# Reordered token loads, paired modulation products and rearranged feed-forward buffers in a hybrid pooling and attention layer

## The chip, the cores and the metric

The kernel runs on one core of one Trainium2 chip. The metric is device time in microseconds (us) of one execution: 905.08 us before the change, the median of 3 runs (904.38 to 905.84).

## The reference, cut to what matters

One layer works on 640 tokens of width 1024: 128 context tokens (`x_prompt`) and 512 latent tokens (`x_sample`, a grid of 8 rows by 64 columns). All numbers are fp32.

```python
shift, scale, gate = split(silu(cond) @ w_mod + b_mod)    # two conditions: latent and context
h = rms(x) * g * (1 + scale) + shift
z = h @ w_in                                  # pooling channels, q, k, v and two gates
x1 = x + gate * ((pool_branch * sigmoid_a + attention_branch * sigmoid_b) @ w_out)
h2 = rms(x1) * g2 * (1 + scale2) + shift2
u = h2 @ w_up                                 # 2 x 2816 features
cv = conv3(u)                                 # width-3 depthwise convolution over tokens
y = x1 + gate2 * ((silu(cv[:, :2816]) * cv[:, 2816:]) @ w_down)
```

The outputs are y for both kinds of tokens and the new k and v of the context.

## The kernel before, in words

There are 128 partitions. Channels come in 8 tiles of 128 (`kt`), tokens in 5 tiles of 128 (`t`; tile 0 is the context, tiles 1 to 4 are latent), features in 22 tiles (`f`). An fp32 operand is split into a high part (a cast to fp32r on ScalarE) and a low part (operand minus high part, on VectorE); a product is three matmuls: high times high, high times low, low times high. The helper `split_to` (L132 to L134) makes the pair: L133 is the cast, L134 the subtraction. A tile scheduler sets each engine's order from the program's order and its own estimate of when things are due; `tc.keep_in_program_order`, `tc.issue_after` and `add_manual_dep` pin single instructions.

The stages, by where they lie in the trace:

- **0 to 140 us, start and projections.** `load_x` (L254) loads the token tiles: the context contiguously (L256), the latent tiles through `xl_blocks` (L251), which gives partition p of a block the tokens of a 16-column strip of the grid: from one grid row to the next the address moves on by 64 tokens, 256 KB. `normalise` (L271) squares and sums a tile on ScalarE (L275), takes the root (L277) and the reciprocal (L279), scales (L280), and TensorE transposes it (L284). `mod_rows` (L142) makes shift and scale for one channel tile: two weight tiles `in_wm` of 512 KB, 8 matmuls by the condition `cz` (L149) into one PSUM tile, and a copy to `mrows` (L152); `mod_scale_shift` (L155) turns the rows into columns with two products by the two-column selector `sel` (L157, L158). `make_h` (L292) writes the modulated h^T, split. The v product runs over the channel tiles (`tok_step`, L203 to L205). The raw weight tiles here share `SRAW` = 6 buffers.
- **140 to 400 us.** Attention, pooling, gates and merge. The change does not touch their code.
- **400 to 457 us, output projection and second norm.** `out_product(t)` (L727) makes the second half of the output columns for token tile t (L745 to L747); `residual` (L717) multiplies by the gate, adds to `x1` and squares. The row statistics follow (L751 to L754); `xn` is x1 times the reciprocal root (L756, ScalarE, 128x1024, one buffer). `second_h(t-1)` (L762) is called in the middle of the product of tile t: 8 transposes of `xn` against the identity (L768), 8 modulations from PSUM (L773 on ScalarE, L776 on VectorE), splits into `b1h`, `b1l` and others. `second_h(4)` stands behind the last product. `sums` (L796) forms differences of quarters of h2^T in three pieces.
- **457 to 850 us, feed-forward.** h2^T is a 2 by 2 block matrix, and for f from 1 on 7 block products take the place of 8, at the price of sums of weights (`weight_sums`, L817, four 128x512 operations on GpSimd) and of activations. `plain` makes f = 0, `up_a` and `up_b` with `products_b` the others (all their matmuls are L865). The convolution (L953 to L955) uses the buffers `ua` (2) and `ug` (1). A group of two f's is multiplied by the down weights (`down_group`, L998; matmuls L994 to L996). `down_weights` (L977) loads 512 KB tiles into `raw`, three buffers shared with the up weights, and splits them into `dhi` and `dlo`.
- **850 to 903 us, the last four f's.** `down_last` (L1010) works through 11 pieces of the output. Each loads its x1 from DRAM into one of three `xr` buffers (L1029) and takes three steps: PSUM plus `acc` (L1031), times the gate `gfb` (L1032), plus `xr` (L1033; pieces 0 to 6 on GpSimd, the others on VectorE), then the store (L1035).

Of the kernel before, what the change touches and what calls it, by code (L numbers as in the profile page):

```python
# [36 lines left out]
SRAW = 6  # L37
# [3 lines left out]
MID = 4  # L41
CUT = 256
# [22 lines left out]
def body(ctx, tc, A):  # L65
# [22 lines left out]
    sel = const.tile([P, 2], F32, name="sel")  # L88
# [42 lines left out]

    def split_to(raw, hi, lo):  # L132
        nc.scalar.copy(hi, raw)  # L133
        return nc.vector.tensor_tensor(out=lo, in0=raw, in1=hi.bitcast(F32), op=SUB)  # L134
# [7 lines left out]
    def mod_rows(chunk, rp):  # L142


        ps = ps_small()
        for half in range(2):
            r = load_raw(A["wm"][2 * chunk + half], rp)
            for k4 in range(4):
                nc.tensor.matmul(ps[32 * k4:32 * k4 + 32, :256], lhsT=cz[:, half * 4 + k4, :],  # L149
                                 rhs=r[:, k4 * 256:(k4 + 1) * 256], start=(half == 0), stop=(half == 1))  # L150
        rows = rp.tile([P, 256], F32, tag="mrows", name="mrows", bufs=2)
        nc.scalar.copy(rows, ps[:, :256])  # L152
        return rows

    def mod_scale_shift(kt, rows):  # L155
        ps = ps_small()
        nc.tensor.matmul(ps[:, 0:2], lhsT=rows[:, :P], rhs=sel, start=True, stop=True)  # L157
        nc.tensor.matmul(ps[:, 2:4], lhsT=rows[:, P:], rhs=sel, start=True, stop=True)  # L158
        nc.vector.tensor_scalar(out=mS[:, 0, kt, :], in0=ps[:, 0:2], scalar1=vec[:, V_BSA + kt:V_BSA + kt + 1],
                                scalar2=None, op0=ADD)  # L160
        nc.vector.tensor_scalar(out=mA[:, 0, kt, :], in0=ps[:, 2:4], scalar1=bca1[:, kt:kt + 1],
                                scalar2=vec[:, V_GM + kt:V_GM + kt + 1], op0=ADD, op1=MULT)
# [87 lines left out]

    xl_blocks = A["xl"].rearrange("(r t c) d -> t c r d", r=ROWS, c=16)  # L251
    junk = hlo.rearrange("p a b -> p (a b)")

    def load_x(t):  # L254
        if t == 0:
            nc.sync.dma_start(xts[0], A["xc"])  # L256
        else:
            nc.sync.dma_start(xts[t], xl_blocks[t - 1])
# [4 lines left out]
    def split_wv():  # L263
# [3 lines left out]
        tc.keep_in_program_order(nc.scalar.copy(hi, r))  # L267
        nc.gpsimd.tensor_tensor(out=lo, in0=r, in1=hi.bitcast(F32), op=SUB)
# [34 lines left out]
    rows = {0: mod_rows(0, sp)}  # L303
    for t in range(3):
        load_x(t)
    rows[0] = mod_scale_shift(0, rows[0])
# [11 lines left out]
    rows[1] = mod_rows(1, sp)  # L318
    make_h(0, done * P, T)
    mod_scale_shift(1, rows.pop(1))  # L320
    acc = ps_five()
    for kt in range(KT):
        if kt % 2 == 1 and kt < KT - 1:
            split_wv()
        if kt + 2 < KT:
            rows[kt + 2] = mod_rows(kt + 2, sp)
        if kt % 2 == 0 and kt < KT - 2:
            load_wv()
        if kt + 1 < KT:
            make_h(kt + 1)  # L330
        if kt + 2 < KT:
            mod_scale_shift(kt + 2, rows.pop(kt + 2))
# [383 lines left out]

    def residual(ps, t, chunk, sq):  # L717
# [5 lines left out]
        else:  # L723
            nc.vector.tensor_tensor(out=x1[:, t, sl], in0=x1[:, t, sl], in1=tmp, op=ADD)
        nc.scalar.activation(tmp, x1[:, t, sl], AF.Square, accum_out=sq[:, t:t + 1])
# [13 lines left out]
    def out_product(t, mid):  # L739
# [13 lines left out]
        nc.scalar.activation(std, std, AF.Sqrt, bias=eps, scale=1.0 / D)  # L753
        nc.vector.reciprocal(std, std)  # L754
# [7 lines left out]
    def second_h(t, xn):  # L762
# [71 lines left out]
    for t in range(5):  # L834
        xns.append(out_product(t, lambda t: second_h(t, xns[t])))
        if t == 3:
            sums(*J[0])
# [312 lines left out]
```

## Time and profile before

| | |
|---|---|
| median of 3 runs | 905.08 us |
| the profiled execution | 904.5 us |
| its span in the trace | 902.7 us |
| TensorE matmul (PE) | 864.6 us, 96% of the span |
| TensorE weight load (PEld) | 778.1 us, 86% |
| VectorE (DVE) | 663.9 us, 74% |
| ScalarE (ACT) | 394.3 us, 44% |
| GpSimd (POOL) | 227.1 us, 25% |
| DMA | 112.20 MB, mean 124 GB/s |

PE is TensorE's matmuls, PEld its weight loads, which overlap them; SPq is the DMA queue that SyncE issues into. The trace names an instruction by its line, its engine, the tile written and the tiles read, and gives the idle time before it with what ended that.

### The profile page before, as it was taken

The page shows a single profiled execution, that of the slowest core. Times are in us where ns is not written, and L with a number is a line of the kernel's source. Part 1 is how long each engine was busy: PE and PEld are TensorE (multiplying, and loading weights), DVE is VectorE, ACT ScalarE, POOL GpSimd, SP SyncE. Part 2 cuts the span into 40 slices and gives each one's busy share as a digit, 9 for nine tenths or more (in the row PEclk, how much of TensorE's full clock was granted, in tenths as well). Part 3 has the DMA queues.
Part 4 walks back from the last instruction along what each step waited for, and adds up shares of the span by engine and source line. Part 5 has one row for each costly group of instructions (what it writes and reads, how often), then busy time and mean ns, then how long its engine had stood idle before and what let it go on. Part 6 is the DMA issues. An engine that isn't in the chain of part 4 may idle for free.

```text
span 902.7 us, 13356 instructions
## 1 busy us (share of the span) xinstructions
PE 864.6 (96%) x5234; PEld 778.1 (86%) x5234; DVE 663.9 (74%) x1003; ACT 394.3 (44%) x711; POOL 227.1 (25%) x176
## 2 busy tenths in 40 slices
PE   3999999999998999999999899999999999999897
PEld 2778898887898999987799799999989999898885
DVE  2657986897479733544799778879797887978767
ACT  4441245444443323223775553535445353444540
POOL 2121000000000021322016423354332444423304
PEclk9999999999999999999999999999999999999999
DMA  9859425674364222255213321213222121312206
GB/s 252 304 195 272 138 77 176 199 227 135 100 206 158 84 79 73 71 214 183 95 46 138 131 74 67 94 47 99 89 94 88 53 94 50 127 59 94 94 0 198
DMA packets 33023, 112.20 MB, mean 124 GB/s; under 512 B 3856, under 2 KB 4528, under 8 KB 32704
## 3 DMA queue, kind: packets, MB, share of 16 engines
q1 hardware_dynamic: 31840, 107.91, 35.9%
q0 software_dynamic: 1120, 3.44, 1.3%
q8 instruction: 41, 0.67, 0.3%
q14 instruction: 22, 0.18, 0.1%
HBM read 104.50 MB, written 5.78 MB: 122 GB/s over the span
## 4 chain that ended last, share of the span: by engine, by line
PE 82%; DVE 7%; DMA 5%; ACT 3%; issue 2%; SPq 0%; POOL 0%; DVEq 0%; ACTq 0%; POOLq 0%
PE acc L865 25%; PE acc L219 21%; PE sm L995 5%; PE sm L996 5%; PE sm L994 4%; PE acc L203 4%; PE acc L205 4%; PE acc L204 4%; DVE wlo L134 2%; DMA raw<-in_wdn 2%; DMA na<-in_xl 2%; ACT whi L133 2%; PE sm L543 1%; PE sm L527 1%; PE sm L505 1%
## 5 line engine op out<-in xcount | busy, mean ns | idle before, releaser
L133 ACT CAST whi<-raw 128x1024 fp32r<-128x1024 f32 (+1 forms) x86 | 81.2, 946 | 192.8 <-PE acc L865 84.3
L134 DVE TENSOR_TENSOR wlo<-raw,whi 128x1024 fp32r<-128x1024 f32 (+1 forms) x86 | 102.5, 1192 | 37.5 <-ACT whi L133 36.6
L865 PE MATMUL acc<-th,whi 128*128 128x322 f32 (+1 forms) x336 | 103.8, 313 | 4.3 <-ACT whi L133 3.0
L865 PE MATMUL acc<-tl,whi 128*128 128x322 f32 (+1 forms) x336 | 104.5, 311 | 0.0
L865 PE MATMUL acc<-th,wlo 128*128 128x322 f32 (+1 forms) x336 | 104.2, 311 | 0.0
L219 PE MATMUL acc<-hhi,whi 128*128 128x320 f32 x320 | 91.0, 318 | 0.4 <-ACT t L442 0.4
L219 PE MATMUL acc<-hlo,whi 128*128 128x320 f32 x320 | 88.9, 311 | 0.0
L219 PE MATMUL acc<-hhi,wlo 128*128 128x320 f32 x320 | 88.1, 311 | 0.0
L819 POOL TENSOR_TENSOR ws<-raw 128x512 f32<-128x512 f32 x21 | 31.3, 1493 | 199.1 <-DMA raw<-in_wup 88.5
L995 PE MATMUL sm<-dlo,ahi 128*128 128x512 f32 (+1 forms) x188 | 73.9, 393 | 0.3 <-DVE dlo L134 0.3
L994 PE MATMUL sm<-dhi,ahi 128*128 128x512 f32 (+1 forms) x188 | 71.2, 394 | 2.5 <-ACT dhi L133 2.5
L996 PE MATMUL sm<-dhi,alo 128*128 128x512 f32 (+1 forms) x188 | 71.4, 394 | 0.0
L865 PEld LDWEIGHTS acc<-th,whi 128*128 128x128 f32 x336 | 63.0, 189 | 7.5 <-ACT whi L133 5.0
L865 PEld LDWEIGHTS acc<-tl,whi 128*128 128x128 f32 x336 | 63.4, 189 | 1.5
L865 PEld LDWEIGHTS acc<-th,wlo 128*128 128x128 f32 x336 | 63.3, 189 | 1.1
L133 ACT CAST whi<-ws 128x1024 fp32r<-128x1024 f32 x42 | 43.0, 1046 | 41.8 <-PE acc L865 41.7
L1008 DVE TENSOR_TENSOR acc<-sm,acc 128x512 f32<-128x512 f32 x80 | 53.3, 683 | 9.5 <-PE sm L996 9.2
L219 PEld LDWEIGHTS acc<-hhi,whi 128*128 128x128 f32 x320 | 57.7, 189 | 2.8 <-issue 1.5
L219 PEld LDWEIGHTS acc<-hlo,whi 128*128 128x128 f32 x320 | 57.6, 188 | 0.8 <-issue 0.7
L865 PE MATMUL acc<-b1h,whi 128*128 128x322 f32 x184 | 57.4, 316 | 0.5 <-ACT b1h L133 0.5
L219 PEld LDWEIGHTS acc<-hhi,wlo 128*128 128x128 f32 x320 | 57.1, 188 | 0.7 <-issue 0.5
L134 DVE TENSOR_TENSOR wlo<-ws,whi 128x1024 fp32r<-128x1024 f32 x42 | 51.6, 1248 | 8.2 <-ACT whi L133 8.2
(295 smaller groups left out, 2244.7 us busy)
## 6 DMA issues: line engine op xcount, KB each, us to landing
raw<-in_wup SPq DMA_DIRECT2D x44, 512.0 KB, 4.0
mw<-in_wmT SPq DMA_DIRECT2D x32, 512.0 KB, 4.2
raw<-in_wdn SPq DMA_DIRECT2D x22, 512.0 KB, 3.6
raw<-in_wmt SPq DMA_DIRECT2D x20, 512.0 KB, 3.5
raw<-in_wm SPq DMA_DIRECT2D x16, 512.0 KB, 4.6
raw<-in_wtok SPq DMA_DIRECT2D x12, 512.0 KB, 7.9
bias<-in_bias SPq DMA_DIRECT2D x16, 384.0 KB, 3.7
raw<-in_wab SPq DMA_DIRECT2D x8, 512.0 KB, 3.5
```

The lines of the kernel that those rows point to most:

```text
L133: nc.scalar.copy(hi, raw)
L134: return nc.vector.tensor_tensor(out=lo, in0=raw, in1=hi.bitcast(F32), op=SUB)
L203: nc.tensor.matmul(ps[t], lhsT=xh, rhs=wh, start=(kt == 0), stop=False)
L204: nc.tensor.matmul(ps[t], lhsT=xh, rhs=wl, start=False, stop=False)
L205: nc.tensor.matmul(ps[t], lhsT=xl, rhs=wh, start=False, stop=(kt == KT - 1))
L219: nc.tensor.matmul(o[:, :n], lhsT=w[:, k], rhs=cut(x, k, c, n), start=st and a, stop=sp and b)
L819: first = nc.gpsimd.tensor_tensor(out=s[:, 1], in0=a21, in1=a22, op=ADD).ins
L865: upped[0] = nc.tensor.matmul(ps[:, cs], lhsT=a[:, c], rhs=b[:, k, cs], start=start and first, stop=last, skip_group_check=skip and not st ...
L994: nc.tensor.matmul(ps, lhsT=xh, rhs=hi[:, sl], start=first and j == js[0], stop=False)
L995: nc.tensor.matmul(ps, lhsT=xh, rhs=lo[:, sl], start=False, stop=False)
L996: nc.tensor.matmul(ps, lhsT=xl, rhs=hi[:, sl], start=False, stop=last and j == js[-1])
L1008: nc.vector.tensor_tensor(out=o, in0=ps, in1=o, op=ADD)
```

## The change

- **Token loads.** The host lays the latent tokens out once more as `xb`, in the column order of h^T, so that each tile is one contiguous 512 KB block; the loads keep program order, and the context and the first latent tile go ahead of the modulation weights. `SRAW` goes from 6 to 9. `split_wv` works in halves.
- **Modulation by pairs.** Channel tiles 0 and 1 stay single. From tile 2 on two tiles share one PSUM tile, one copy and two four-column products; `sel` grows to 6 columns.
- **Second norm.** In place of `xn` and its transposes, ScalarE writes the diagonal matrix `dg` (identity times the reciprocal root, 128x128, two buffers), and the product of x1 and `dg`, an fp32 matmul, transposes and scales at once. `second_h(4)` moves into `plain`'s second product. The sums come in two pieces, one of 64 and one of 258 columns. `behind` adds order between instructions without a semaphore.
- **Weight sums** for f = 2 and 3 move from GpSimd to VectorE.
- **Buffers of the feed-forward.** `ug` gets two buffers. The down weights get a buffer of their own, `dr` (one); the last four alternate between `dr` and `raw`, and their casts go behind the last cast of `up_w`.
- **Last pieces.** All 11 pieces of x1 are loaded ahead into `b1h` and `b1l`, behind the last load of `dr`. The pieces from 6 on have `acc` times gate plus x1 formed on VectorE before their matmuls are done; then PSUM times gate and one addition finish them. Pieces 0 to 5 keep three steps, the third on GpSimd.

```diff
-SRAW = 6
+SRAW = 9
+PRE = 6
...
-    def mod_rows(chunk, rp):
-        ps = ps_small()
+    def mod_rows(c0, n, rp):
+        ps, m = ps_small(), 4 // n
         for half in range(2):
-            r = load_raw(A["wm"][2 * chunk + half], rp)
+            rs = [load_raw(A["wm"][2 * (c0 + j) + half], rp) for j in range(n)]
             for k4 in range(4):
-                nc.tensor.matmul(ps[32 * k4:32 * k4 + 32, :256], lhsT=cz[:, half * 4 + k4, :],
-                                 rhs=r[:, k4 * 256:(k4 + 1) * 256], start=(half == 0), stop=(half == 1))
+                for j, r in enumerate(rs):
+                    g = 32 * (m * j + k4 % m)
+                    nc.tensor.matmul(ps[g:g + 32, :256], lhsT=cz[:, half * 4 + k4, :],
+                                     rhs=r[:, k4 * 256:(k4 + 1) * 256], start=half == 0 and k4 < m,
+                                     stop=half == 1 and k4 >= 4 - m)
...
-            nc.sync.dma_start(xts[t], xl_blocks[t - 1])
+            tc.keep_in_program_order(nc.sync.dma_start(xts[t], A["xb"][t - 1]))
...
-        xn = fp.tile([P, D], F32, name="xn2", bufs=1)
-        nc.scalar.activation(xn, x1[:, t, :], AF.Copy, scale=std)
-        return xn
+        dg = fp.tile([P, P], F32, name="dg", bufs=2)
+        chain["diagonal"] = nc.scalar.activation(dg, ident, AF.Copy, scale=std).ins
+        return dg
...
-                nc.tensor.transpose(pt[:, k * P:(k + 1) * P], xn[:, (q * 4 + k) * P:(q * 4 + k + 1) * P], ident)
+                i = nc.tensor.matmul(pt[:, k * P:(k + 1) * P], lhsT=x1[:, t, (q * 4 + k) * P:(q * 4 + k + 1) * P],
+                                     rhs=dg, start=True, stop=True).ins
...
+        eng = nc.vector if f in (2, 3) else nc.gpsimd
...
-us = {n: [fw.tile([P, TC], F32, name=f"u{n}{j}") for j in range(b)] for n, b in (("a", 2), ("g", 1))}
+us = {n: [fw.tile([P, TC], F32, name=f"u{n}{j}") for j in range(2)] for n in "ag"}
...
-            r = load_raw(A["wdn"][g * GRP + j])
+            if g < NG - 1 or j % 2 == 0:
+                r = fr.tile([P, D], F32, name="dr", bufs=1)
+                loaded[0] = nc.sync.dma_start(r, A["wdn"][g * GRP + j]).ins
+            else:
+                r = load_raw(A["wdn"][g * GRP + j])
...
+        for i, (t, c, w) in enumerate(pieces):
+            behind(nc.sync.dma_start(place(i)[2], xscr[:, t, c:c + w]).ins, loaded[0])
...
+        for i in range(PRE, len(pieces)):
+            o, gate, x = place(i)
+            behind(nc.vector.tensor_tensor(out=o, in0=o, in1=gate, op=MULT).ins, split_last[0])
+            nc.vector.tensor_tensor(out=o, in0=o, in1=x, op=ADD)
...
-            xr = fr.tile([P, 512], F32, tag="xr", name="xr", bufs=3)[:, :w]
-            nc.sync.dma_start(xr, xscr[:, t, sl])
-            o = acc[:, t, sl]
-            nc.vector.tensor_tensor(out=o, in0=ps, in1=o, op=ADD)
-            nc.vector.tensor_tensor(out=o, in0=o, in1=gfb[:, 1 if t == 0 else 0, sl], op=MULT)
-            (nc.gpsimd if i < 7 else nc.vector).tensor_tensor(out=o, in0=o, in1=xr, op=ADD)
+            o, gate, x = place(i)
+            if i < PRE:
+                nc.vector.tensor_tensor(out=o, in0=ps, in1=o, op=ADD)
+                nc.vector.tensor_tensor(out=o, in0=o, in1=gate, op=MULT)
+                nc.gpsimd.tensor_tensor(out=o, in0=o, in1=x, op=ADD)
+            else:
+                tmp = fr.tile([P, AC], F32, name="cv", bufs=3)[:, :w]
+                nc.vector.tensor_tensor(out=tmp, in0=ps, in1=gate, op=MULT)
+                nc.vector.tensor_tensor(out=o, in0=o, in1=tmp, op=ADD)
```

How the order of instructions moves, at three places (a row names the line, the operation, the tile written and what it reads; x2 is a repeat):

On SyncE's queue at the start, before (`vv` and `na` hold the token tiles, `raw` the weights):

```order
L87 DMA vec<-in_vec 128x262
L126 DMA raw<-in_wm 128x1024 x2
L256 DMA vv<-in_xc 128x1024
L258 DMA vv<-in_xl 128x1x1024 x2
L126 DMA raw<-in_wtok 128x1024
L258 DMA na<-in_xl 128x1x1024 x2
```

The same queue after the change:

```order
L88 DMA vec<-in_vec 128x262
L267 DMA vv<-in_xc 128x1024
L269 DMA vv<-in_xb 128x1024
L127 DMA raw<-in_wm 128x1024 x2
L269 DMA vv<-in_xb 128x1024
L127 DMA raw<-in_wtok 128x1024
L269 DMA na<-in_xb 128x1024 x2
```

Two token tiles now stand ahead of the first two modulation weights; the last two stay behind the first tile of v's weights.

On ScalarE in the steady state (one group of down weights, as it repeats), after the change (`dhi` is the high part of a down weight, `dr` its single raw buffer):

```order
L140 CAST dhi<-dr 128x1024
L140 CAST whi<-raw 128x1024
L981 ACTIVATE cv<-ua_4535,vec 128x642
L936 COPY u_6037<-acc 128x320
L140 CAST dhi<-dr 128x1024
```

Three instructions lie between the two casts that use `dr`, where before the casts read from three buffers.

On ScalarE near the end, before:

```order
L970 ACTIVATE cv<-cv 128x642
L133 CAST dhi<-raw 128x1024
L889 COPY p_8219<-acc 128x322
L133 CAST dhi<-raw 128x1024
L133 CAST whi<-ws 128x1024
L133 CAST whi_8309<-ws 128x1024
```

After the change:

```order
L1000 ACTIVATE cv<-cv 128x642
L906 COPY p_8200<-acc 128x322
L140 CAST whi<-ws 128x1024
L140 CAST whi_8290<-ws 128x1024
L939 COPY p_8235<-acc 128x320
L140 CAST ahi<-cv 128x642
L981 ACTIVATE cv<-ua_4534,vec 128x642
L936 COPY u_8315<-acc 128x320
L1000 ACTIVATE cv<-cv 128x642
L140 CAST whi_8298<-raw 128x512
L140 CAST dhi<-dr 128x1024
L140 CAST dhi<-raw 128x1024
```

The casts of the last down weights now stand behind the casts of the summed weights `ws` instead of ahead of them.

## Rows read from the trace of the kernel before

**Rows 1.** Page, busy time, share and instructions of each engine.

```profile
PE 864.6 (96%) x5234; PEld 778.1 (86%) x5234; DVE 663.9 (74%) x1003; ACT 394.3 (44%) x711; POOL 227.1 (25%) x176
```

**Rows 2.** Waits of PE: line, tile, releaser: us in total, times, longest us.

```profile
PE sm L149 <- DMA raw<-in_wm: 7.3, 2, 5.2
...
PE acc L865 <- ACT whi L133: 3.0, 3, 2.4
PE sm L994 <- ACT dhi L133: 2.5, 1, 2.5
...
PE sm L768 <- ACT xn L756: 1.8, 1, 1.8
PE acc L865 <- DVE wlo L134: 1.7, 1, 1.7
PE acc L865 <- DVE ug L920: 1.3, 1, 1.3
...
PE sm L768 <- ACT hf L773: 1.0, 1, 1.0
```

**Rows 3.** Windows: stretch, us, busy (x) PE PEld DVE ACT POOL, clock, DMA share, GB/s.

```profile
9.00:21.00 12.00, 7.02 (x35) 5.63 (x28) 5.66 (x13) 6.12 (x12) 1.33 (x2) 1.00 1.04 244
21.00:27.00 6.00, 3.95 (x15) 3.39 (x16) 2.88 (x7) 3.83 (x9) 2.02 (x2) 0.73 1.03 379
...
453.00:457.00 4.00, 3.88 (x15) 3.71 (x16) 4.00 (x11) 4.00 (x10) 0.00 (x0) 0.61 0.43 170
...
540.00:850.00 310.00, 309.37 (x1813) 286.85 (x1812) 254.63 (x287) 141.85 (x204) 128.28 (x80) 1.00 0.24 80
850.00:866.00 16.00, 12.30 (x82) 11.78 (x81) 12.77 (x17) 10.22 (x15) 0.71 (x1) 1.00 0.21 67
```

**Rows 4.** Chain that ended last, at the start: start us, us, what.

```profile
5.01 16.03 DMA na<-in_xl
```

**Rows 5.** Timeline of PE at one channel tile's modulation: start us, us, instruction.

```profile
48.19 0.28 PE L157 MATMUL sm<-sel,mrows 128*128 128x2 f32 x2
...
48.33 0.36 PE L158 MATMUL sm<-sel,mrows 128*128 128x2 f32 x2
...
48.62 1.07 PE L149 MATMUL sm<-raw,cz 128*32 128x256 f32 x16
```

**Rows 6.** Timeline of PE: eight transposes of xn and the matmul behind them.

```profile
434.46 1.03 PE L768 MATMUL sm<-ident,xn 128*128 128x128 f32 x8
...
435.25 0.48 PE L747 MATMUL acc<-w1h,mlo 128*128 128x512 f32 x1
```

**Rows 7.** Timeline of PE in attention: six fp32 products, two records each.

```profile
210.55 0.88 PE L543 MATMUL sm<-pT,vv 128*64 128x128 f32 x12 [0.62 <-DVE mx L510]
```

**Rows 8.** Timeline of DVE beside GpSimd's weight sums for f = 2.

```profile
477.22 2.29 DVE L134 TENSOR_TENSOR wlo<-raw,whi 128x1024 fp32r<-128x1024 f32 x1
```

**Rows 9.** Groups of DVE, 852 to 903 us: count, busy, mean ns, idle before.

```profile
L134 DVE TENSOR_TENSOR dlo<-raw,dhi 128x1024 fp32r<-128x1024 f32 x1 | 1.2, 1225 | 0.4 <-ACT dhi L133 0.4
```

**Rows 10.** Timeline of ACT at 621 us, steady state.

```profile
621.43 1.05 ACT L133 CAST whi<-raw 128x1024 fp32r<-128x1024 f32 x1 [1.34 <-PE acc L865]
622.38 0.93 ACT L953 ACTIVATE cv<-ua,vec 128x642 f32<-128x642 f32 x1
```

**Rows 11.** Page, DMA issues: count, KB each, median us to landing.

```profile
raw<-in_wdn SPq DMA_DIRECT2D x22, 512.0 KB, 3.6
```

**Rows 12.** Timeline of DVE and PE in the last 30 us.

```profile
873.74 0.83 DVE L134 TENSOR_TENSOR tl<-cv,th 128x642 fp32r<-128x642 f32 x1 [0.80 <-ACT th L133]
...
882.97 0.68 DVE L1031 TENSOR_TENSOR acc<-acc 128x512 f32<-128x512 f32 x1
...
884.89 0.68 DVE L1031 TENSOR_TENSOR acc<-sm,acc 128x512 f32<-128x512 f32 x1
...
895.68 0.28 PE L996 MATMUL sm<-whi,tl 128*128 128x256 f32 x1
...
899.39 0.42 DVE L1033 TENSOR_TENSOR acc<-acc,xr 128x256 f32<-128x256 f32 x1
```

More of the change, by code (lines that the diff above doesn't have):

```diff
@@ L130, in load_raw, with behind @@
         return r
+    def behind(i, other):
+        tc.add_manual_dep(i, other.name,
+                          mybir.DependencyInfo(mybir.DependencyClass.NoSync, mybir.DependencyReason.DATA),
+                          reason="order")
     def split_to(raw, hi, lo):
-        nc.scalar.copy(hi, raw)
-        return nc.vector.tensor_tensor(out=lo, in0=raw, in1=hi.bitcast(F32), op=SUB)
+        a = nc.scalar.copy(hi, raw)
+        return a.ins, nc.vector.tensor_tensor(out=lo, in0=raw, in1=hi.bitcast(F32), op=SUB)
     def load_w(src, own=None):
@@ L302, in body @@
     wv, wr = [], []
[L303 to L306, printed above, removed]
+    load_x(0)
+    load_x(1)
+    first = mod_rows(0, 1, sp)
+    load_x(2)
+    mod_scale_shift(0, 1, first)
     load_wv()
@@ L317, in body @@
             done = t + 1
-    rows[1] = mod_rows(1, sp)
+    second = mod_rows(1, 1, sp)
     make_h(0, done * P, T)
-    mod_scale_shift(1, rows.pop(1))
+    mod_scale_shift(1, 1, second)
     acc = ps_five()
@@ L715, in body @@
     w1l = wo.tile([P, KT, 512], F32R, name="w1l")
+    chain = {}
     def residual(ps, t, chunk, sq):
@@ L784, in second_h, with sums @@
                 h, l = (b2h, b2l) if q else (b12h, b12l)
-                split_to(hf[:, ks, s0:c1], h[:, :, s0 - HB:c1 - HB], l[:, :, s0 - HB:c1 - HB])
-    def sums(j0, j1):
+                chain["cast"], j = split_to(hf[:, ks, s0:c1], h[:, :, s0 - HB:c1 - HB], l[:, :, s0 - HB:c1 - HB])
+                chain["low"] = j.ins
+        return i
+    def sums(j0, j1, order=None):
         b11, b21 = hf[:, 0:4, j0:j1], hf[:, 4:8, j0:j1]
         b12, b22 = hf[:, 0:4, HB + j0:HB + j1], hf[:, 4:8, HB + j0:HB + j1]
-        nc.vector.tensor_tensor(out=b11, in0=b12, in1=b11, op=SUB)
+        i = nc.vector.tensor_tensor(out=b11, in0=b12, in1=b11, op=SUB).ins
+        if order:
+            behind(i, order)
         nc.vector.tensor_tensor(out=b12, in0=b22, in1=b12, op=SUB)
@@ L932, in plain @@
             product(ps, wa, x1_, slice(0, n), start=True, more=True)
-            product(ps, wb, x2_, slice(0, n), skip=False)
+            if mid and u is not us["a"][0]:
+                turned.append(mid())
+                with tc.issue_after(turned[0]):
+                    product(ps, wb, x2_, slice(0, n), skip=False)
+            else:
+                product(ps, wb, x2_, slice(0, n), skip=False)
             nc.scalar.copy(u[:, c0:c0 + n], ps[:, :n])
-    plain(B11, B21, HB, 1)
-    sums(*J[1])
-    up_a(1)
+    plain(B11, B21, HB, 1, lambda: second_h(4, dgs[4]))
+    sums(0, 64, chain["root"])
+    with tc.issue_after(turned[0]):
+        up_a(1)
     plain(B12, B22, H2C, 1 + HB)
-    summed_h = sums(*J[2])
-    for j in ((0, 192), (192, HB)):
-        split_sums(*j)
+    summed_h = sums(64, HB, chain["low"])
+    split_sums(0, HB)
     up_w(1)
```

119 lines of the change are left out of this document (67 added, 52 removed).

## The prediction

> **What bounds the kernel now.** I read the busy times first: TensorE's matmuls are busy 864.6 of 902.7 us [rows 1], so at most 38 us of idle can go, unless matmuls themselves go. Next the windows and the waits of PE, to see where the idle lies and who ends it. From 540 to 850 us PE is busy 309.37 of 310 us [rows 3]: nothing can be won there by a buffer or an order, only lost. Idle is at the start, at the second norm, and at the end. At the start (9 to 27 us) PE is busy 7.02 of 12 us and then 3.95 of 6; the DMA engines are full all that time (share 1.04 and 1.03), but move 244 GB/s in the first stretch and 379 in the second [rows 3], and the chain of waits sits for 16.03 us on the last latent token tile, which ends at 21.07 [rows 4]. The longest wait of PE, 7.3 us, is also for a load there [rows 2]. Around 450 us PE waits 1.8 us for `xn` and 1.0 for the modulated `hf` [rows 2], and then runs at a granted clock of 0.61 for 4 us, between the two levels of 1.2 and 2.4 GHz [rows 3]. Near 500 us it waits once for the first down weight's cast, 2.5 us [rows 2], and around 853 and 866 us up to 2.4 us for a cast (`whi`) and 1.3 us for `ug` [rows 2]; the window 850 to 866 has 3.7 us of PE idle [rows 3]. After the last matmul the end takes 899.81 - 895.96 us of VectorE steps and 2.9 us of store [rows 12].
>
> All sums are against the profiled execution of 904.5 us; the median of the runs stands 0.6 above it. A measurement of this kernel tells about 0.2%, 1.8 us, from no change.
>
> **The start.** The bytes stay the same: the four latent tiles are loaded from another array, as whole blocks. In 9 to 21 us 12.0 us at 244 GB/s moved 2.93 MB; at the 379 GB/s of the stretch behind it (in which no latent tile is left after 21.07) they would take 7.7 us, 4.3 less [rows 3, 4]. Two token tiles pass two modulation weights on SyncE's queue, so the first modulation matmuls start later; they fall into idle time, for PE waits 5.2 us on one of those loads and 2.1 on the other [rows 2]. I take off 0.3 for it: **-4.0 us**. The ends are 0 (the rate does not depend on the layout) and -5.0 (all idle of 9 to 21 us). What follows is covered by PE's own work, since the v product is then what bounds; the three extra raw buffers and the halved split hang on that and cost nothing.
>
> **Modulation by pairs.** The matmuls by `cz` stay as many. Six channel tiles become three pairs, so three groups of selector products go: from 48.19 to 48.62 us such a group holds PE for 0.43 us [rows 5]. Four columns instead of two cost next to nothing, as the two products' time is not their two columns. 3 x 0.43 = **-1.3 us**. The pair needs four weight tiles instead of two before it ends; the end above is one block of 16 matmuls coming late once, +1.1 (1.07 us, [rows 5]); below, -1.3.
>
> **Second norm.** 40 transposes become 40 fp32 products. Eight transposes hold PE from 434.46 to 435.25, 0.099 us each [rows 6]. For an fp32 product of 128 weights' columns the nearest row is the selector pair: two in 0.43 us, 0.215 each [rows 5]; the products of attention with 64 weight columns and 128 moving ones take 0.88 / 6 = 0.147 [rows 7]. I take 0.215, since the weights here have 128 columns as in the selector products: 40 x (0.215 - 0.099) = +4.6. The ends are 0.147 (+1.9) and the two added, 0.36, if loading weights and moving columns don't overlap (+10.5). What goes: ScalarE writes 128x128 instead of 128x1024 per tile, into two buffers, so PE's waits of 1.8 and 1.0 should go; and `second_h(4)` in the middle of `plain` fills the gap ahead of it. With the gap goes the low clock: 4.0 us at 0.61 cost 4.0 x 0.39 = 1.6 [rows 2, 3]. The first down weight has its own buffer and no up weight ahead of it: -2.5 [rows 2]. Sum: 4.6 - 2.8 - 1.6 - 2.5 = **-2.3 us**.
>
> The weight sums of f = 2 and 3 add 8 x 0.68 = 5.4 us to VectorE (a 128x512 step there takes 0.68, [rows 12]), but take GpSimd's away from beside it: with them a 1024-column subtraction takes 2.29 us, without them 1.23 [rows 8, 9], so 1.06 is lost on each of the operations there. I set them against each other, at **0**; the wait of 1.7 us for a `wlo` [rows 2] may go or double, so the ends are -1.7 and +1.7. The sums in two pieces are work of VectorE beside PE's products: 0, on the same cover.
>
> **Steady state.** PE idles 0.63 us in 310 [rows 3]: a second `ug` and another buffer for down weights can win nothing: **0**. A second cast from the same `dr` must wait for the first subtraction and a reload; if the cover is gone, that is a cost (third rival).
>
> **The end.** PE's two waits near 853 and 866 should go: the casts of `ws` no longer stand behind two casts that wait for loads, and `ug` has a second buffer. That is 2.4 + 1.3 = 3.7 us earlier for PE [rows 2]. But VectorE decides the end. Behind the last split (873.74 + 0.83 = 874.57, [rows 12]) it gets 5 products and 5 additions ahead: 2 x (3 x 0.68 + 2 x 0.42) = 5.8. Then six pieces with two steps each beside GpSimd: 884.89 - 882.97 = 1.92 each, 11.5. Then five pieces with two steps: 5.8 again. 23.1 us. From 874.57 that ends at 897.7, 2.1 before 899.81. The split itself comes earlier with PE, by 3.7 at most; VectorE has 16 - 12.77 = 3.2 us of idle in 850 to 866 [rows 3], but waits there for ScalarE's part too, so I take half, 1.8: **-3.9 us**. The eleven x1 pieces (2.6 MB, 6.9 us at 379 GB/s) land beside the last up products, ahead of their use, and the loads of `xr` between the stores go. The ends are 0 (what goes from the end is eaten by the added steps and late loads) and -6.7 (PE ends at 892.3, and 0.84 for two steps behind it).
>
> **Sum.** -4.0 - 1.3 - 2.3 - 3.9 = -11.5: 893.0 profiled, **893.6** as a median.
>
> **The rivals.**
> *Everything hides.* The start gives -5.0, the fp32 products cost 0.147 each (2.7 less), and the end is PE's (2.8 more): 893.6 - 1.0 - 2.7 - 2.8 = 887.1. For it: the waits all lie in a few places; against it: VectorE's 23.1 us are counted from its own rows. 0.13.
>
> *The loads are not faster.* Then the start gives 0 and the time is 893.6 + 4.0 = 897.6. For it: weights and tokens share the engines, and the weights may be what is slow in 9 to 21 us; against it: the rate rises to 379 as the last latent tile lands [rows 3, 4]. 0.13. The Trainium skill ("DMA: Bandwidth & Descriptors", section "Latency and other measured facts") bears on this rival: it finds 207 GB/s at a row pitch of 512 KiB against 214 in full, and a loss only from 2 MiB on, and the pitch here is 256 KB. By that rule the layout is worth nothing; the trace so far, 244 against 379 GB/s, speaks against it.
>
> *The single buffer `dr` stalls the steady state* (slower than before). Between the two casts from `dr` ScalarE has a cast of 1.05 and a convolution of 0.93 us and a copy [rows 10]; the reload needs the subtraction, 1.2, and 3.6 to land, 4.8 [rows 9, 11]. If ScalarE has no other pause, each of nine groups loses 4.8 - 2.0 = 2.8 us, 25.2 in all: 918.8. It decides as soon as ScalarE's wait holds up a cast that PE is about to need. Against it: ScalarE waits 1.34 us for PE right there [rows 10], is busy only 141.85 of 310 us [rows 3], and the cast behind the second one is for the last product of the five. 0.08.
>
> *The change does not do what it says at two places:* loads as slow as before (+4.0), and the waits of the norm and the first down weight come back under other names (2.8 + 1.6 + 2.5 = +6.9): 904.5, no change. 0.06.
>
> **How the numbers follow.** The forecast has 0.60, the others 0.13, 0.13, 0.08 and 0.06. The forecast's own ends reach from about 885 (every term at its lower end) to 902 (the products at 0.36 and the pairs at +1.1). The range 886 to 902 holds the forecast and the first two rivals but for the corners, and leaves out the last two, 0.14. Faster than 903.3: 0.60 + 0.13 + 0.13 = 0.86; the same: 0.06; slower than 906.9: 0.08.
>
> **What would show it.** Start: the last token tile lands near 17 us, at over 300 GB/s from 9 us on, and v's first matmul near 19 instead of 23. Pairs: three selector groups from tile 2 on. Norm: no wait of PE for `dg` above 0.5 us, clock 1.00 at 453 to 457, products 0.2 us apart. Steady state: PE idle under 1 us from 540 to 840. End: no PE wait above 1 us from 850 on, and from there to the end of the span 4 us less than now. The prediction is wrong if PE waits for `dhi` or for a cast behind it in the steady state, if the first 20 us still run at 250 GB/s, or if VectorE starts the last pieces later than PE delivers them by more than 3 us.

## The result, and the profile after

The change makes the kernel faster, by half of what was forecast or less: 901.21 us median of 13 runs (900.24 to 904.1) against 906.83 (904.38 to 913.75) for the kernel before, ratio 0.9939 with a 95% interval of 0.9921 to 0.9957. A second, later measurement gave 904.15 against 907.44, ratio 0.9961 (0.9941 to 0.9981). Forecast were 893.6 us and a gain of 11.5; the gains measured are 5.6 and 3.3. Of the two medians, 901.21 lies inside the stated 886 to 902 and 904.15 outside.

The two profiled executions are both off their medians, in opposite directions: the one before took 904.5 us at a mean granted clock of 0.995 (its runs average 0.990), the one after 903.9 at 0.991 (its runs 0.994). Their spans, 902.7 and 902.1 us, hardly differ (0.6 us), so the comparison below goes stretch by stretch.

Page of the kernel after, busy times; they answer to [rows 1]:

```profile
PE 870.8 (97%) x5262; PEld 784.5 (87%) x5262; DVE 683.6 (76%) x1009; ACT 391.7 (43%) x708; POOL 224.9 (25%) x173
```

VectorE has 20 us more to do. Waits of PE after the change (us, times, longest), which answer to [rows 2]:

```profile
PE sm L158 <- DMA raw<-in_wm: 8.7, 1, 8.7
PE sm L1032 <- DVE acc L1046: 2.5, 7, 0.4
PE acc L232 <- ACT pdh L140: 2.5, 1, 2.5
PE acc L880 <- ACT p L939: 1.8, 2, 1.0
PE sm L555 <- DVE mx L522: 1.5, 2, 0.9
...
PE acc L216 <- ACT hhi L311: 1.3, 2, 0.9
PE sm L1032 <- DVE acc L1044: 1.2, 1, 1.2
```

The waits for `xn`, `hf`, `ug`, the first down weight and `wlo` are gone. New are eight waits for an `acc` that VectorE has not read yet (2.5 us in seven, 1.2 in one), and two for `p`. Windows after the change, which answer to [rows 3] (columns as there: stretch, us, busy of PE, PEld, DVE, ACT, POOL, clock, DMA share, GB/s):

```profile
9.00:21.00 12.00, 9.46 (x54) 7.25 (x47) 5.99 (x15) 7.27 (x17) 3.64 (x4) 0.91 1.03 397
...
170.00:190.00 20.00, 18.75 (x114) 15.82 (x114) 15.65 (x42) 8.12 (x27) 0.00 (x0) 0.83 0.54 176
262.00:284.00 22.00, 19.54 (x123) 19.28 (x122) 22.00 (x38) 8.19 (x16) 1.43 (x8) 0.92 0.66 217
453.00:457.00 4.00, 4.00 (x31) 4.00 (x30) 3.52 (x9) 2.89 (x8) 0.33 (x8) 1.00 0.18 76
540.00:850.00 310.00, 307.52 (x1798) 284.64 (x1797) 267.37 (x283) 141.87 (x201) 134.08 (x79) 1.00 0.24 79
600.00:700.00 100.00, 99.33 (x590) 92.68 (x589) 87.45 (x91) 48.47 (x69) 43.28 (x26) 1.00 0.26 85
850.00:866.00 16.00, 15.27 (x102) 14.82 (x102) 11.66 (x16) 9.37 (x14) 1.58 (x1) 1.00 0.20 64
```

The start now runs at 397 GB/s, the chain waits 10.5 us for the last token tile instead of 16.0 [rows 4], and the low clock at 453 is gone. But the clock falls in two new places in attention, and the steady state idles 2.5 us instead of 0.6. The same three new windows of the kernel before:

```profile
170.00:190.00 20.00, 19.56 (x148) 16.57 (x147) 18.19 (x48) 9.93 (x32) 0.00 (x0) 1.00 0.67 215
262.00:284.00 22.00, 19.60 (x134) 19.33 (x133) 22.00 (x38) 9.55 (x20) 1.32 (x5) 1.00 0.64 216
600.00:700.00 100.00, 99.73 (x593) 92.92 (x592) 81.23 (x91) 48.32 (x69) 39.54 (x25) 1.00 0.26 84
```

Chain at the start of the kernel after:

```profile
4.08 10.52 DMA na<-in_xb
```

Landmarks (start of the first or last such matmul in the trace, us), the change in the stretch between one and the next (minus is shorter), and in the last column the landmarks of the fastest kernel of the experiments:

| | before | after | change in the stretch up to it | `raw`, casts free |
|---|---|---|---|---|
| first gate product (after start, v, q, k) | 122.4 | 118.2 | -4.2 | 117.9 |
| first pooling product (`pdh`) | 273.5 | 273.4 | +4.1 | 272.7 |
| first output projection | 389.9 | 391.3 | +1.5 | 390.6 |
| first product of `products_b` with the summed activations (`th`) | 473.6 | 473.6 | -1.4 | 473.1 |
| last such product, f = 21 (the last up product) | 867.7 | 867.0 | -0.7 | 864.6 |
| end of the span | 902.7 | 902.1 | +0.1 | 897.7 |

### The profile page after: what moved, and what is told of

Read it like the earlier page. It is cut to its first block, busy times and chain, and to the rows that moved or that the text cites. A ratio compares the mean times of both kernels' runs of the same rounds, so it can differ in the third digit from the quotient of the medians.

```text
span 902.1 us, 13408 instructions
## 1 busy us (share of the span) xinstructions
PE 870.8 (97%) x5262; PEld 784.5 (87%) x5262; DVE 683.6 (76%) x1009; ACT 391.7 (43%) x708; POOL 224.9 (25%) x173
## 3 DMA queue, kind: packets, MB, share of 16 engines
q1 hardware_dynamic: 31840, 107.91, 35.1%
## 4 chain that ended last, share of the span: by engine, by line
PE 75%; DVE 15%; issue 5%; DMA 3%; ACT 2%; SPq 0%; DVEq 0%; ACTq 0%
PE acc L232 21%; PE acc L880 20%; DVE wlo L141 5%; PE acc L216 4%; PE acc L218 4%; PE acc L217 4%; PE sm L1032 4%; PE sm L1033 4%; PE sm L1034 3%; DVE cv L982 2%; PE sm L555 1%; PE sm L539 1%; DMA na<-in_xb 1%; PE sm L517 1%; PE acc L760 1%
## 5 line engine op out<-in xcount | busy, mean ns | idle before, releaser
L141 DVE TENSOR_TENSOR wlo<-raw,whi 128x1024 fp32r<-128x1024 f32 (+1 forms) x85 | 106.8, 1256 | 38.5 <-ACT whi L140 37.9
L232 PE MATMUL acc<-hhi,whi 128*128 128x320 f32 x320 | 93.1, 323 | 0.4 <-ACT t L454 0.4
L232 PE MATMUL acc<-hlo,whi 128*128 128x320 f32 x320 | 90.9, 316 | 0.0
L232 PE MATMUL acc<-hhi,wlo 128*128 128x320 f32 x320 | 90.2, 317 | 0.0
L1032 PE MATMUL sm<-dhi,ahi 128*128 128x512 f32 (+1 forms) x188 | 73.4, 399 | 3.9 <-DVE acc L1046 2.5
L1001 POOL TENSOR_TENSOR cv<-cv 128x642 f32<-128x642 f32 x21 | 35.2, 1677 | 158.1 <-DVE cv L983 121.5
L141 DVE TENSOR_TENSOR wlo<-ws,whi 128x1024 fp32r<-128x1024 f32 x42 | 62.3, 1499 | 8.5 <-ACT whi L140 8.5
```

Source lines behind the costliest of these rows:

```text
L141: return a.ins, nc.vector.tensor_tensor(out=lo, in0=raw, in1=hi.bitcast(F32), op=SUB)
L232: nc.tensor.matmul(o[:, :n], lhsT=w[:, k], rhs=cut(x, k, c, n), start=st and a, stop=sp and b)
L1001: (nc.vector if f == NF - 1 else nc.gpsimd).tensor_tensor(out=a, in0=a, in1=b, op=MULT)
L1032: nc.tensor.matmul(ps, lhsT=xh, rhs=hi[:, sl], start=first and j == js[0], stop=False)
```

## The experiments

Each run has its mean granted clock, and time and clock go together: within the kernels of this study, 0.63 us per 0.001 (one slope fitted to all their runs, each kernel about its own mean). The last column moves every run to 0.995 by that slope, and gives the mean and its standard error. Single kernels have slopes from 0.2 to 1.2, and the two measurements of the changed kernel give 901.7 and 902.5, so differences below 1 us there mean little. Rows were measured on several chips; the ratio is always to the kernel before on the same chip.

| kernel | runs | median us | ratio to before (95%) | mean clock | us at 0.995 |
|---|---|---|---|---|---|
| before | 117 | 907.05 | | 0.9902 | 904.3 +- 0.2 |
| changed (two measurements) | 25 | 901.21, 904.15 | 0.9939, 0.9961 | 0.9938 | 902.1 +- 0.2 |
| before with contiguous blocks (two) | 24 | 903.68, 903.77 | 0.9953 (0.9927 to 0.9979), 0.9966 (0.9943 to 0.9990) | 0.9912 | 901.3 +- 0.4 |
| changed, gathered loads | 12 | 904.77 | 0.9978 (0.9956 to 0.9999) | 0.9947 | 905.1 +- 0.6 |
| changed, single modulation | 12 | 902.51 | 0.9948 (0.9928 to 0.9967) | 0.9939 | 901.7 +- 0.5 |
| changed, sums on GpSimd | 12 | 908.78 | 1.0011 (0.9993 to 1.0030) | 0.9888 | 905.1 +- 0.3 |
| changed, one `ug` | 6 | 901.88 | 0.9931 (0.9906 to 0.9956) | 0.9952 | 901.7 +- 0.5 |
| the same with `xn` | 12 | 904.45 | 0.9964 (0.9943 to 0.9985) | 0.9929 | 902.6 +- 0.4 |
| changed, `raw` for three last weights | 12 | 903.03 | 0.9949 (0.9928 to 0.9971) | 0.9935 | 901.9 +- 0.4 |
| changed, no steps ahead | 12 | 904.30 | 0.9965 (0.9942 to 0.9988) | 0.9929 | 902.8 +- 0.4 |
| both of these | 12 | 905.06 | 0.9969 (0.9950 to 0.9989) | 0.9929 | 903.8 +- 0.3 |
| changed, `raw` for all | 8 | 902.24 | 0.9937 (0.9915 to 0.9959) | 0.9925 | 900.8 +- 0.3 |
| the same, one `ug` | 12 | 905.43 | 0.9986 (0.9965 to 1.0007) | 0.9924 | 903.9 +- 0.5 |
| changed, `raw` for all, casts free (two) | 13 | 901.05, 900.33 | 0.9924 (0.9891 to 0.9956), 0.9919 (0.9888 to 0.9949) | 0.9928 | 898.8 +- 0.4 |
| the same, single modulation | 12 | 903.16 | 0.9941 (0.9915 to 0.9966) | 0.9930 | 901.1 +- 0.6 |

### The start

**Gathered loads in the changed kernel.**

```diff
-            tc.keep_in_program_order(nc.sync.dma_start(xts[t], A["xb"][t - 1]))
+            tc.keep_in_program_order(nc.sync.dma_start(xts[t], xl_blocks[t - 1]))
```

> Edit: the changed kernel with the latent tiles gathered from x_sample as before (rows of a tile 256 KB apart), all else as changed, order of loads included. Theory (the layout sets the rate): from 8 to 20 us the DMA moves about 250 GB/s instead of 400, the last token tile lands near 21 us instead of 14.6, the first transposes of z start 4 us later (114.5 instead of 110.4), and the time is 4 us longer: ratio near 0.998. Rival (a pitch of 256 KB costs nothing, the order of loads and the pairs made the gain): the rate stays at 400 GB/s and the ratio at 0.994.

Window of this kernel:

```profile
9.00:21.00 12.00, 7.86 (x44) 5.28 (x44) 5.17 (x13) 5.36 (x12) 1.62 (x2) 0.99 1.04 294
```

With the same order of loads the rate drops from 397 to 294 GB/s, and the first gate product comes at 122.2, against 118.2 changed and 122.4 before: the layout makes all of the start's gain. The forecast's rival, that the loads are not faster, falls. What about the layout does it, the 256 KB between rows or the order of the rows, was not separated.

**Contiguous blocks alone, in the kernel before, run twice.**

```diff
-            nc.sync.dma_start(xts[t], xl_blocks[t - 1])
+            nc.sync.dma_start(xts[t], A["xb"][t - 1])
```

> Edit: the kernel before, with the latent tiles laid out as contiguous blocks and nothing else. Theory (the layout alone speeds the start by some 4 us, but the stretch of attention gives part of it back: PE's waits for `mx` and `pdh` grow and the granted clock falls after them): first transposes of z 3 to 4 us earlier (about 111 against 114.6), the first pooling product (`pdh`) only 0 to 2 us earlier than 273.5, ratio 0.996 to 0.999. Rival (what is won at the start is kept): `pdh` near 270 and ratio about 0.995 or below.

> Edit: the kernel before with the contiguous blocks alone, once more. Theory: ratio 0.996, granted clock about 0.991 as in the kernel before. Rival: ratio above 0.998, its first result was luck.

The first gate product came at 118.0 and 116.5, 4.4 and 5.9 us earlier; `pdh` at 270.4 and 268.9, 3.1 and 4.6 earlier. So 1.3 us were lost in attention each time, with no fall of the clock ahead of `pdh`, and most was kept: the rival (`pdh` near 270, ratio about 0.995) is nearer than the theory. The second run repeats the ratio (0.9966) and the clock (0.9916). At equal clock the layout alone is worth 3.0 us; the whole change is worth 2.2. Everything else in the change adds up to +0.8 us there, which is not told apart from nothing, while its higher mean clock (0.9938 against 0.9912) would give 1.6 back.

**Modulation tile by tile, nine buffers kept.**

```diff
-            pair = mod_rows(kt + 2, 2, sp)
+            pair = mod_rows(kt + 2, 1, sp)
```

> Edit: the changed kernel with modulation tile by tile, nine raw buffers and contiguous loads kept. Theory (the forecast's term of 1.3 us for three groups of products): the stretch from the first v product to the first gate product grows by 1 to 1.5 us from 97.8, ratio 0.995 to 0.996. Rival (pairs only move the waiting: the start's gain came from the loads alone, since the run with the gather gave back all 4.0 us): no change within 0.5 us in that stretch.

> Edit: the same with modulation tile by tile. Theory (pairs are worth nothing, the first v products just start 1 us later while PE idles 1.3 us less behind them): equal to the run with pairs within 0.7 us. Rival (the forecast's 1.3 us): 1.3 us slower.

From the first v product to the first gate product it took 97.1 us, against 97.8 in pairs, 0.8 of which is a fall of the clock: no gain from the pairs in this stretch. In the changed kernel a four-column pair of products costs what a two-column pair did (0.43 us from 33.14 to 33.57, PE's timeline), so three groups are saved:

```profile
33.14 0.28 PE L167 MATMUL sm<-sel,mrows 128*128 128x4 f32 x2
33.28 0.36 PE L168 MATMUL sm<-sel,mrows 128*128 128x4 f32 x2
33.57 1.48 PE L158 MATMUL sm<-raw,cz 128*32 128x256 f32 x18
```

but PE then idles 1.3 us in the v product, waiting for `hhi`; tile by tile it idles 0.1 there. The second of these runs, with the last buffers of this section, was 2.3 us slower than with pairs at equal clock, with errors of 0.4 and 0.6, where the theory had 0.7 at most and the rival 1.3; its end had another fall of the clock, behind a wait of PE of 3.65 us for `whi`. What pairs do to the rest stays open.

### The second norm and the weight sums

**`xn` and transposes again** (with one `ug`, which makes room; compared with the run with one `ug`).

```diff
-        chain["diagonal"] = nc.scalar.activation(dg, ident, AF.Copy, scale=std).ins
+        chain["diagonal"] = nc.scalar.activation(dg, x1[:, t, :], AF.Copy, scale=std).ins
...
-                i = nc.tensor.matmul(pt[:, k * P:(k + 1) * P], lhsT=x1[:, t, (q * 4 + k) * P:(q * 4 + k + 1) * P],
-                                     rhs=dg, start=True, stop=True).ins
+                i = nc.tensor.transpose(pt[:, k * P:(k + 1) * P], dg[:, (q * 4 + k) * P:(q * 4 + k + 1) * P],
+                                        ident).ins
```

> Edit: the kernel with one `ug`, and in the second norm `xn` (128x1024 on ScalarE, one buffer) and the transposes again; `second_h` of the last tile stays inside the second product of `plain` (the single `ug` makes room in memory, so it is compared with that run). Theory (an fp32 product costs 0.216 us against 0.099, and the move of `second_h` alone removes the waits): PE is busy 4.6 us less, the waits for `xn` stay under 1.5 us, so this run is 2 to 4 us faster than the one with one `ug`. Rival, the forecast's sum (`dg` is what removes the waits of 2.8 us and the low clock of 1.6): those come back, and the two runs are equal within 0.5 us.

The theory was wrong and the forecast's reading right. The waits of PE came back, 2.2 us of the 2.8, and so did the low clock:

```profile
PE sm L783 <- ACT xn L771: 1.2, 1, 1.2
...
PE sm L783 <- ACT hf L789: 1.0, 1, 1.0
```

```profile
453.00:457.00 4.00, 3.63 (x13) 3.36 (x14) 3.50 (x12) 4.00 (x9) 0.00 (x0) 0.62 0.00 0
```

With one `ug` and `dg` the clock in that window is 1.00. The run is 0.9 us slower at equal clock (with errors of 0.4 and 0.5) and 2.6 in the median. The products' price was the forecast's: 12 of them hold PE from 434.56 to 437.15 in the changed kernel, 0.216 us each.

```profile
434.56 2.84 PE L783 MATMUL sm<-dg,x 128*128 128x128 f32 x24
437.15 0.48 PE L760 MATMUL acc<-w1l,mhi 128*128 128x512 f32 x1
```

**Weight sums on GpSimd.**

```diff
-        eng = nc.vector if f in (2, 3) else nc.gpsimd
+        eng = nc.gpsimd
```

> Edit: the changed kernel with the weight sums of f = 2 and 3 on GpSimd again. Theory (the forecast's zero: what VectorE saves in sums it loses in slowed subtractions): no change within 1 us, ratio 0.993 to 0.995, but PE's wait of 1.05 us for `p` at 478 changes its name to `wlo`. Rival (the sums on VectorE are what crowds 457 to 540 us, where VectorE is busy 19.99 of 20 us): PE's idle from 457 to 540 us, 3.2 us now, falls below 1.5 and the ratio to 0.992.

Neither the theory nor the rival came out. This one line costs 3 us at equal clock; by the ratios, 1.0011 against 0.9939 and 0.9961, it is 4.5 to 6.5 in time. PE waits for the cast of the summed activations, in a stretch (457 to 480 us) where GpSimd is now busy 6.9 us and in the changed kernel idle:

```profile
PE acc L880 <- ACT th L140: 3.9, 1, 3.9
```

The sums of activations that this cast reads are VectorE's (`hf`), and they come late: beside GpSimd's weight sums the first takes 2.32 us, in the changed kernel 1.23. In this run, and in the changed kernel:

```profile
467.20 2.32 DVE L818 TENSOR_TENSOR hf<-hf 128x1032 f32<-128x1032 f32 x1
```

```profile
465.83 1.23 DVE L818 TENSOR_TENSOR hf<-hf 128x1032 f32<-128x1032 f32 x1
```

The clock falls behind that wait (0.95 from 457 to 480 us). The kernel before, with its sums on GpSimd too, had no such wait; its activation sums came in three pieces, which may be why (not tried).

### The buffers of the feed-forward and the end

**Three of the last four down weights through `raw`; no steps ahead; both.**

```diff
-            if g < NG - 1 or j % 2 == 0:
+            if g < NG - 1 or j == 0:
```

```diff
-        for i in range(PRE, len(pieces)):
-            o, gate, x = place(i)
-            behind(nc.vector.tensor_tensor(out=o, in0=o, in1=gate, op=MULT).ins, split_last[0])
-            nc.vector.tensor_tensor(out=o, in0=o, in1=x, op=ADD)
```

> Edit: the changed kernel, but of the last four down weights only the first goes through the single buffer `dr`, the other three through the three `raw` buffers. Theory (the reload of `dr` delays the end): ScalarE's wait of 2.62 us for `dr` before the cast at 866.87 goes, the last split `tl`, which ended 877.41 - 867.0 = 10.4 us behind the last up product, ends at most 8 us behind it, and the span from the last up product to the end shrinks by 2.5 to 3.5 us from 35.4: about 898 us, ratio to before near 0.990. Rival (VectorE's own work sets the end whatever lands when): `tl` and the end stay within 0.5 us of their places, ratio 0.994.

> Edit: the changed kernel without the products and additions of acc ahead of the last pieces; all eleven pieces take three steps, as before, x1 still loaded ahead. Theory (VectorE is late at the end, so work put ahead of its first piece costs more than it saves): 5.0 us of steps ahead of the first piece go, five third steps (3 x 0.6 + 2 x 0.35 = 2.5 us) come back, so VectorE ends 1.5 to 2.5 us sooner: ratio about 0.992. Rival, the forecast's assumption (the steps ahead are free, since VectorE is idle before PE delivers): the end comes 2.5 us later, ratio about 0.997.

> Edit: both edits together, three last down weights through `raw` and no steps ahead. Theory: with the split early, VectorE has time ahead of the first piece, so here the steps ahead were worth their place: this run is slower than the one with `raw` alone, by 1 to 2 us, and the first piece waits for PE again. Rival (the steps ahead always cost): this run is the fastest of the four, below 0.989.

What the theories speak of, in ScalarE's timeline of the changed kernel: the cast from `dr` frees it late, and the next one waits for the reload.

```profile
860.79 1.04 ACT L140 CAST dhi<-dr 128x1024 fp32r<-128x1024 f32 x1
...
866.87 1.05 ACT L140 CAST whi<-dr 128x1024 fp32r<-128x1024 f32 x1 [2.62 <-DMA dr<-in_wdn]
```

and in VectorE's: the last split, and the last step.

```profile
876.58 0.83 DVE L141 TENSOR_TENSOR tl<-cv,th 128x642 fp32r<-128x642 f32 x1 [0.80 <-ACT th L140]
...
898.75 0.42 DVE L1089 TENSOR_TENSOR acc<-acc,cv 128x256 f32<-128x256 f32 x1
```

With `raw` the wait went, and the split stood 9.0 us behind the last up product instead of 10.4; the span from there to the end shrank from 35.1 to 33.7 us, 1.4 instead of 2.5 to 3.5. PE lost 0.9 of it ahead, at a wait for `p` (1.7 us, 0.73 before), because the casts still stood together in front of that copy. At equal clock that is 0.2 us (901.9 against 902.1): nothing. Without the steps ahead the end grew by 1.0 us (36.1), with `raw` by 2.3 (36.0 against 33.7): the steps ahead save more than they cost. That refutes the theory of the second run, bears out that of the third, and agrees with the forecast's assumption, at 1.0 us instead of the 2.5 that it was put at.

**All down weights through `raw`; one `ug`; both; `raw` with the casts free.**

```diff
-            if g < NG - 1 or j % 2 == 0:
-                r = fr.tile([P, D], F32, name="dr", bufs=1)
-                loaded[0] = nc.sync.dma_start(r, A["wdn"][g * GRP + j]).ins
-            else:
-                r = load_raw(A["wdn"][g * GRP + j])
+            r = wp.tile([P, D], F32, tag="raw", name="raw", bufs=3)
+            loaded[0] = nc.sync.dma_start(r, A["wdn"][g * GRP + j]).ins
```

```diff
-    ua, ug = us["a"][f % 2], us["g"][f % 2]
+    ua, ug = us["a"][f % 2], us["g"][0]
```

```diff
-            if g == NG - 1:
-                behind(i, last_cast[0])
```

> Edit: the changed kernel with all down weights through the three shared `raw` buffers again; the rest as changed (order of the last casts, second `ug`, loads ahead). Theory (the own buffer `dr` moves its subtraction beside GpSimd's weight sums, VectorE falls behind and PE waits 2.5 us in seven pieces for an `acc` that VectorE has not read yet): these seven waits go, and VectorE's busy time from 600 to 700 falls from 87 back to some 82 us; the wait of 2.5 us for the first down weight near 500 comes back, so the time changes by less than 1 us either way (ratio 0.993 to 0.995). Rival (the second `ug` reorders VectorE, `dr` is innocent): the seven waits stay and the 2.5 us near 500 come on top, ratio about 0.997.

> Edit: the changed kernel with one `ug` buffer. Theory (`dr` makes the waits): the waits for `acc` stay near 2.5 us, and PE waits again for `ug` near 866, about 1.3 us: ratio 0.995. Rival (the second `ug` makes them): they go, VectorE's busy time from 600 to 700 falls to 82 us, ratio 0.991.

> Edit: the changed kernel with all down weights through `raw` and one `ug`: the buffers of the feed-forward as before. Theory (the two buffer edits win nothing once the sums stand on VectorE): within 1 us of the changed kernel at the same granted clock, no waits for `acc`, PE's wait of 1.4 us for `ug` near 866 back. Rival (the two buffers together carry the gain of the last stretch): the stretch from the last b1 product to the end, 51.1 us in the changed kernel, goes back to 53 or 54.

> Edit: the changed kernel with all down weights through `raw`, and the casts of the last four no longer held behind the last cast of `up_w`, so that the scheduler puts two of them ahead of the casts of the weight sums again. Theory (that order was what made PE wait 2.4 us near 853 before): PE waits there again for `whi`, 1 to 2.5 us, and the time grows by that against the run with `raw` alone (900.3 us at a granted clock of 0.996), ratio about 0.995. Rival (the order is worth nothing, the second wait moves with it): equal within 0.5 us.

The seven waits for `acc` stay with one `ug` (2.5 us) and go with `raw`: `dr` makes them. Window of the run with `raw` for all, and one group of VectorE, the subtraction for the low part of the activations, in the changed kernel and in this one (600 to 700 us; busy, mean ns of one):

```profile
600.00:700.00 100.00, 99.71 (x592) 92.86 (x591) 80.40 (x92) 47.44 (x68) 39.42 (x25) 1.00 0.26 84
```

```profile
L141 DVE TENSOR_TENSOR alo<-cv,ahi 128x642 fp32r<-128x642 f32 x5 | 7.0, 1407 | 2.7 <-ACT ahi L140 2.7
```

```profile
L141 DVE TENSOR_TENSOR alo<-cv,ahi 128x642 fp32r<-128x642 f32 x5 | 4.1, 821 | 2.7 <-ACT ahi L140 2.7
```

Where the time goes shows in the timelines of GpSimd and VectorE in the changed kernel: a weight sum, and the subtraction beside it.

```profile
622.04 1.88 POOL L842 TENSOR_TENSOR ws<-raw 128x512 f32<-128x512 f32 x1
```

```profile
623.09 1.92 DVE L141 TENSOR_TENSOR wlo<-raw,whi 128x1024 fp32r<-128x1024 f32 x1
```

With `dr` the order on VectorE moves. Between 600 and 700 us the five subtractions `wlo` of 1024 columns from `raw` fall beside GpSimd's weight sums and take 1.95 us instead of 1.23; those for `alo` take 1.41 on average instead of 0.82, and those from `ws`, three of which fall beside GpSimd's product `cv`, 1.56 instead of 1.22. With `raw` VectorE is back at 80 us. The first down weight did not wait in either kernel: `dr` was not what removed that 2.5 us, and what did stays open.

With one `ug` and `raw` together PE waits 3.8 us for `ug` near the end, and the stretch from the last b1 product to the end is 54.8 us, as the rival has it. So with `raw` the second `ug` is worth 3 us; with `dr` it is worth nothing (901.7 us with one, 902.1 with two).

Freeing the last casts did not cost what was expected. PE waited 2.1 us for `whi` again, as the theory has it, but the last split came 8.6 us behind the last up product instead of 10.4, and the run was the fastest so far.

**That kernel again, beside the changed kernel again.**

> Edit: none, the changed kernel once more, beside the three others on one chip. Theory (layout alone carries the gain in time, the rest only saves falls of the granted clock): at equal clock equal to the kernel before with contiguous blocks, within 1 us; in ratio 0.001 to 0.003 better, about 0.994. Rival (the rest gains in time too): 2 us or more better at equal clock.

> Edit: the changed kernel with all down weights through `raw` and the last casts free, once more. Theory (`dr` and the held casts eat 2 to 3 us: seven waits for `acc`, and the last split 3 us late): 2 to 3 us below the changed kernel beside it, ratio 0.991 to 0.992. Rival (chance of seven runs): within 1 us of it.

Same chip: 900.33 against 904.15 us, ratios 0.9919 and 0.9961; at equal clock 898.8 against 902.1 over both measurements. VectorE's timeline of this kernel (span 897.7 us), the last split and the last step:

```profile
872.41 0.83 DVE L141 TENSOR_TENSOR tl<-cv,th 128x642 fp32r<-128x642 f32 x1 [0.80 <-ACT th L140]
...
894.38 0.43 DVE L1084 TENSOR_TENSOR acc<-acc,cv 128x256 f32<-128x256 f32 x1
```

This is the version that beats both: the change with down weights through the three shared buffers, and without the order put on the last casts. `dr` and that order eat 3 us of what the rest of the change wins. On the same chip the layout alone took 903.77 us, the changed kernel 904.15: there the rest of the change, as it stands, won nothing. So the first theory of this pair holds at equal clock (902.1 against 901.3) and misses the 0.001 to 0.003 in the ratio.

## Why the prediction was right in direction and wrong in size

Two of its steps failed. The first is that another buffer for the down weights costs nothing unless its reload stalls: up to the last up product the forecast had 6.0 us of gain, and 2.1 came. The second is "What follows is covered by PE's own work": of the start's 4 us, 1.3 to 4.1 were lost again in attention. By its own terms:

- **The start, -4.0, and the pairs, -1.3.** The first gate product comes 4.2 us earlier, all of it from the layout. The saved groups of the pairs are there, but 1.3 us of idle in front of `hhi` takes them back, about what their upper end (+1.1) allowed for. Then attention has waits of its own: for `mx` on VectorE, and for `pdh`, a cast behind a VectorE that is busy 22.00 of 22 us from 262 to 284. In the first profile everything went, 4.1 us up to `pdh`, of which 0.8 is more idle and 3.4 a fall of the clock; in the second 1.9 went, and in the two runs of the layout alone 1.3, without a fall.
- **The norm, -2.3.** Without the first down weight the forecast was +0.2 (products +4.6, waits -2.8, clock -1.6); the stretch from the output projection to the first summed product is 1.4 shorter. The parts are there: 0.216 us a product (forecast 0.215), no wait, no low clock. But PE had 3.5 us of idle there (389.9 to 453.1) and not 2.8, for the forecast counted the two longest waits alone. The weight sums at 0 were mis-sized: moving them is worth 3 us at equal clock, in this arrangement.
- **The steady state, 0, and PE's two waits near the end, -3.7.** With the 2.5 us of the first down weight the stretch between the first `th` product and the last up product was to shrink by 6.2 us; it shrank by 0.7. The old waits are gone, the first down weight's too, though not through `dr`. But `dr`, which did not stall as the rival of 25 us had it, moved VectorE's subtractions beside GpSimd, and PE waits 2.5 and 1.2 us for `acc`. With `raw` these waits go and the stretch is 391.4 us (393.4 changed, 394.1 before). The waits for `p` are not from `dr`: with `raw` they are still 1.8 us; the one near 863 goes when the last casts are free, the one at 478 stays in every version of the changed kernel but that with the sums on GpSimd. PE's waits in the stretch fall from 8.8 to 6.0 us, yet the time by 0.7 only. There are 11 instead of 7, and a wait costs more than the idle that is listed: around the one at 478.25, listed with 1.05, two matmuls start 1.35 us apart where others start 0.15 apart. The rest of that difference is not accounted for.
- **Behind the last up product.** The forecast had the end 0.2 us closer to it (3.9 less the 3.7 that PE was to gain); it is 0.1 further. VectorE's work behind the last split is 21.8 us (forecast 23.1). But the split, said to come 1.8 us sooner, came 2.8 later (877.41 against 874.57), 10.4 us behind the last up product instead of 6.9. The cast from `dr`, which waited 2.62 us, is part of it: with `raw` for three weights it is 9.0, with `raw` and free casts 8.6, and the stretch to the end 33.1 us instead of 35.1. What makes up the rest, 1.7 us, was not found.
- **The reference point.** All terms were set against one execution at a clock of 0.995, which the text placed 0.6 us under the median of three runs; over 117 runs it is 2.5 under. Of the 4.5 us between the means of all runs, 2.3 go with the changed kernel's higher mean clock (0.9938 against 0.9902, at 0.63 us per 0.001) and 2.2 remain at equal clock. The forecast had 1.6 us of clock, from the one place at 453, in a sum of 11.5. That the first median fell inside the range is in good part this clock, which the sum did not contain.

Which part keeps the clock up is shown in part: the change without its layout has 0.9947, the layout alone 0.9912, the sums on GpSimd take it to 0.9888. Why a wait is followed by a fall in one run and not in the next was not settled.

## What to carry to other kernels

A buffer of its own frees a queue but also moves the work that empties it; look at what that work will run beside, above all for two engines that slow each other, before costing it at nothing. A gain at the start is only kept if the next stretch is bound by the same engine; find the next wait on another engine and price it there. And take the granted clock of each run beside its time: here half of the difference went with the clock, and one profile could not show it.

## What the runs showed of the hardware

- Loads of 128 rows of 4 KB, with 256 KB between one row and the next of the same column, are slower than contiguous blocks with the same other loads around them: from 9 to 21 us the DMA moved 244 GB/s against 385 in the kernel before, and 294 against 397 in the changed one.
- A fall of the granted clock to 0.50 follows short waits, but not each: in the changed kernel PE waited 0.89 us at 177.3 and the clock was at 0.50 from about 179.3 to 186.1, 3.4 us lost; the second profile of the same kernel has the wait and no fall. Behind the wait of 2.5 us for `pdh` it fell in the changed kernel and not in the kernel before, whose wait was 2.4; in the fastest kernel it fell behind one of 2.3, so the length of the wait does not tell. The first 13 runs of the changed kernel fall in two groups: nine at a clock of 0.995 or more took 900.2 to 901.8 us, four below it 903.6 to 904.1.

The second profile of the changed kernel, window of that place:

```profile
170.00:190.00 20.00, 19.14 (x144) 15.71 (x143) 17.13 (x44) 8.23 (x27) 0.00 (x0) 1.00 0.62 196
```
